# A hybrid decoder trunk: low-rank products in pairs on the two row halves, and wider small products at the mixers' seams

## The chip, the cores and the metric

The kernel runs on one core of one Trainium2 chip. The metric is the time of one execution on the device, in microseconds (us). TensorE (PE) multiplies, VectorE (DVE) and ScalarE (ACT) work elementwise, GpSimd (POOL) and SyncE (SP) mostly issue transfers. Products land in the banks of PSUM; everything else is in SBUF or in device memory.

## The reference

Two layers; each is a half-step SwiGLU block, a mixer and another half-step SwiGLU block, with a layer norm after each, on 16 learned tokens and 512 input tokens of width 1024. The mixer adds a convolution branch and an RWKV-7 branch. The part that the change touches, cut to what matters:

```python
def _rwkv_branch(zr, time_mix, w0, w_up, a0, a_up, g_up, k_k, k_a, r_k, lnx_g, lnx_b, wo):
    zr = zr + (_shift(zr) - zr) * time_mix
    r, k, v, zw, za, zg = jnp.split(zr, ...)       # 3 x 1024, then 64, 64, 128 columns
    w = -jax.nn.softplus(-(w0 + jnp.tanh(zw) @ w_up)) - 0.5
    decay = jnp.exp(-jnp.exp(w))                   # = exp(-0.6065 * sigmoid(w0 + ...))
    a = jax.nn.sigmoid(a0 + za @ a_up)             # the rate
    g = jax.nn.sigmoid(zg) @ g_up                  # the gate
    kk = normalised per head (k * k_k)
    k = k * (1.0 + (a - 1.0) * k_a)
    # per head and token, S is 64 x 64:
    #   sa = -S kk ; S = S * decay + sa (kk a)^T + v k^T ; y = S r
    ...
    return y @ wo
```

## The kernel before

Activations stand transposed: 128 partitions hold a slice of the width, the 528 tokens lie along the free dimension, in two halves of 264. Every large product is split into three of type float32r (high x high, high x low, low x high), each with 128 x 128 weights and 264 columns; lines L217 (SwiGLU, output projections) and L246 (input projection of the mixer) issue them. Float32 products have two records each in the trace, a float32r product has one.

The mixer (`mixer`) runs as follows. `mixer_begin` makes the low-rank inputs, then the **low-rank products**: decay (`w_up`, 64 rows, partitions 0 to 63), rate (`a_up`, 64 rows, partitions 64 to 127) and gate (`g_up`, 128 rows), eight output slices `o` each, for two halves of the tokens. One call of `lowrank` is one of them for one `o`: six products, then the evacuation from PSUM (a Sigmoid or Tanh on ACT, a scaling on DVE), then a store. Calls take turns between the two banks of the tile `sc` (emptied by one instruction of 528 columns) and the banks `tr` and `ch` (two of 264). The list LOW sets their order: decay and gate in turn, then the rate. Between them, after every fourth, comes a `filler`: one of the large input projections that the later stages need, whose inputs are ready, so that PE has work.

Then the recurrence, by head quarters q = 0 to 3, in chunks of 64 tokens. `prep` makes the factors (L1144: sums of squares per head, 128 rows, 32 columns; L1156 and L1157: transposes; L1205), `scores` the chunks' score matrices (L1250, L1259: 64 x 128 weights on the two row halves in turn, each half into a bank of its own), `substitution` inverts 16 x 16 blocks on DVE, `inverse` joins them to 64 x 64 (L1333, L1340; the last two of its three rounds L1340 take 32 columns), `meta` does the 16 learned tokens (L1365, L1371, L1459: 16 rows of `small`), `scan` walks through the chunks (L1415, L1428, L1431, L1436). Fillers and convolution taps stand between these. **Seam** here means the place between two quarters, where `inverse`, `meta` and the `prep` after the next stand together.

Engines work in the order of their own queue. The recorded program is reordered by a scheduler that knows priorities and modelled durations, so a change of one instruction moves others.

Of the kernel before, what the change touches and what calls it, by code (L numbers as in the profile page):

```python
# [7 lines left out]
F32 = mybir.dt.float32  # L8
F32R = mybir.dt.float32r
I32 = mybir.dt.int32  # L10
AF = mybir.ActivationFunctionType
# [5 lines left out]
P = 128  # L17
# [3 lines left out]
NM = 16  # L21
# [19 lines left out]
TAIL = 3  # L41
JTAIL = 4
HEAD = 2
LOW = [(j, o) for o in range(8) for j in (0, 2)] + [(1, o) for o in range(8)]
GNACT = ()
YR = (0, 3, 6)
CV = (0, 4, 7, 8)
# [51 lines left out]
class Trunk:  # L99
# [237 lines left out]
    def layer_vectors(self, l, room, mm):  # L337
        nc, lp = self.nc, self.lp
        y, ssum, sq = room
        nat, tmn = ssum[:, 0:P], ssum[0:26, P:2 * P]  # L340

        def fetch(out, src):
            self.nosync(nc.sync.dma_start(out=out, in_=src), self.issued)

        for i, nme in enumerate(VECS):
            src = self.d[nme][l]
            if nme == "r_k":
                src = src.rearrange("h n -> (h n)")
            fetch(nat[i * KT:(i + 1) * KT, :], src.rearrange("(o p) -> o p", p=P))
            if i % 4 == 3:  # L350
                yield True
        fetch(tmn, self.d["time_mix"][l].rearrange("(o p) -> o p", p=P))
        cwn = ssum[0:4 * TAPS, 2 * P:4 * P].rearrange("a (g p) -> a g p", p=P)
        for o in range(KT):
            g, i = divmod(o, 4)
            fetch(cwn[i * TAPS:(i + 1) * TAPS, g], self.d["conv_w"][l][:, o * P:(o + 1) * P])
            if o == 3:
                yield True
        yield True
        vec = lp.tile([P, P], F32, name="vec")  # L360
        ps = mm()
        nc.tensor.transpose(ps[:, 0:P], nat, self.ident)
        nc.tensor.transpose(ps[:, P:P + 26], tmn, self.ident[:26, :26])
        nc.scalar.copy(vec, ps[:, :P])
        tm = lp.tile([P, 26], F32, name="tm")
        nc.scalar.copy(tm, ps[:, P:P + 26])
        omtm = lp.tile([P, 26], F32, name="omtm")
        nc.vector.tensor_scalar(omtm, tm, -1.0, 1.0, op0=ALU.mult, op1=ALU.add)
        ps = mm()
        for g in range(2):  # L370
            nc.tensor.transpose(ps[:, 4 * g * TAPS:4 * (g + 1) * TAPS], cwn[:, g],
                                self.ident[:4 * TAPS, :4 * TAPS])
        cw = lp.tile([P, KT, TAPS], F32, name="cw")
        nc.scalar.mul(cw.rearrange("p o t -> p (o t)"), ps[:, :KT * TAPS], 0.5)
        v8 = lambda x: vec[:, VECS.index(x) * KT:(VECS.index(x) + 1) * KT]
        nkk = lp.tile([P, KT], F32, name="nkk")
        nc.vector.tensor_scalar_mul(nkk, v8("k_k"), -1.0)
        omka = lp.tile([P, KT], F32, name="omka")
        nc.vector.tensor_scalar(omka, v8("k_a"), -0.5, 1.0,
                                op0=ALU.mult, op1=ALU.add)  # L380
        half = lp.tile([P, 2, KT], F32, name="half")
        for i, x in enumerate(("a0", "k_a")):
            nc.vector.tensor_scalar_mul(half[:, i], v8(x), 0.5)
        self.layers.append((vec, tm, omtm, cw, nkk, omka, half))

# [582 lines left out]
    def mixer_begin(self, zs, filler):  # L968
# [14 lines left out]
        nc.vector.scalar_tensor_tensor(xg[1], z, 1.0, xg[0].bitcast(F32), op0=ALU.add,  # L983
                                       op1=ALU.subtract)
        filler(START[0])
        acts = (lambda o: (AF.Sigmoid, self.v1("w0", o), 1.0),
                lambda o: (AF.Tanh, self.half[:, 0, o:o + 1], 0.5))
        up = [(d["w_up"], slice(0, 64)), (d["a_up"], slice(64, P))]

        room = mp.tile([P, 4, KT, P], F32R, name="sb", bufs=1)  # L990
# [1 line left out]
                       dst=[room[:, 0], room[:, 1]])  # L992

        self.bi = 0
        stage = {}

        def lowrank(w, x, o, r, dst, act=None):
            if act is None:
                t = self.tmp("v", 4) if o % 2 else mp.tile([P, NCH * 4, 32], F32, name="b4",
                                                           bufs=B4)  # L1000
                t = t if o % 2 else t.rearrange("p a b -> p (a b)")[:, 0:T]
            else:
                if o == 0:
                    stage[r.start] = self.rows().rearrange("p q e f t -> p (q e f) t")
                t = stage[r.start][:, o]
            both = self.sc() if self.bi % 2 == 0 else None
            self.bi += 1
            for h in range(2):
                s = slice(h * (T // 2), (h + 1) * (T // 2))
                pm = (self.sm(("tr", "ch")[h]) if both is None else both[:, h])[:, :T // 2]  # L1010
                for j, (a, b) in enumerate(((0, 0), (0, 1), (1, 0))):
                    nc.tensor.matmul(pm, w[a][r, o, :], x[b][r, s], start=j == 0, stop=j == 2)
                to = t[:, s]
                if both is not None:
                    if h == 0:
                        continue
                    pm, to = self.pv(both), self.tv(t)
                if act is None:
                    nc.vector.tensor_scalar_mul(to, pm, 0.5)
                else:  # L1020
                    f, b, scale = act(o)
                    nc.scalar.activation(to, pm, f, bias=b, scale=scale)
            nc.sync.dma_start(out=dst[o * P:(o + 1) * P, :], in_=t)

        wg = self.wunit(d["g_up"][self.l].rearrange("r (o c) -> r o c", c=P),
                        dst=[room[:, 2], room[:, 3]])
        todo = [[lambda o=o, r=r, act=act, dst=dst: lowrank(w, x, o, r, dst, act)
                 for o in range(KT)]
                for (_, r), act, dst in zip(up, acts, (self.ds, self.as_))]
        todo.append([lambda o=o: lowrank(wg, xg, o, slice(0, P), self.ggs) for o in range(KT)])  # L1030
        for i, (j, o) in enumerate(LOW):
            todo[j][o]()
            if i % LOWSTEP == LOWSTEP - 1:
                filler(1)
            self.taps(TAP0[0])
        filler(START[1])
        self.sb = mp.tile([P, NCH, 4, 2 * C], F32, name="sb", bufs=1)

        self.ut = mp.tile([P, NCH * 2, C], F32, name="ut")

        small = mp.tile([NM, 2048], F32, name="small")
        self.small, o = {}, 0
        for name, n in (("kb", 512), ("s", 256), ("v", 256), ("u", 256), ("y0", 256), ("y1", 256), ("y2", 256)):
            self.small[name] = small[:, o:o + n]
# [70 lines left out]
    def prep_pair(self, q, p, Q):  # L1115
# [22 lines left out]

        pn = self.sc()
        pn, p0 = pn[:, 0], pn[:, 1]  # L1140
        tr = p0[:, NM:NM + 160]
        for j in range(5):
            k0 = NM + j * P if j < 4 else 0
            nc.tensor.matmul(tr[:, 32 * j:32 * j + 32], sq[:, k0:k0 + P], self.bones[:, ::4],  # L1144
                             start=True, stop=True)
        tr = tr[:, ::16]
        rs = mp.tile([P, 10], F32, name="rs", bufs=1)
        rx = self.tmp()[:, :4 * P].rearrange("p (j h v) -> p j h v", j=4, h=2)
        rx0 = mp.tile([P, P], F32, name="rx", bufs=1)[0:NM].rearrange("a (h v) -> a h v", h=2)
# [64 lines left out]
    def scores(self, q, Q):  # L1214
# [7 lines left out]
                nc.tensor.transpose(tr[0:NM, f * 256 + p * P:f * 256 + (p + 1) * P],  # L1222
                                    FB[p][:, f * NM:(f + 1) * NM], self.ident)
        kb0 = self.small["kb"]
        nc.scalar.copy(kb0, tr[0:NM, :])
        Q["kb0"] = kb0.rearrange("p (f h v) -> p f h v", f=2, h=4)
        ps = self.sc()
        ps = [ps[:, 0], ps[:, 1]]
# [2 lines left out]
        for e in range(2):  # L1231
            p0 = ps[e][0:NM, 0:4 * 2 * NM].rearrange("a (p f x) -> a p f x", p=2, f=2)
            r = slice(HS * e, HS * e + HS)
            for p in range(2):
                for f in range(2):
                    nc.tensor.matmul(p0[:, p, f, :], FB[p][r, f * NM:(f + 1) * NM],
                                     G[r, p, 1, :, 0:NM], start=True, stop=True)
            nc.vector.tensor_tensor(s0[:, e].rearrange("a p f g t -> a (p f) g t"),
                                    ps[e][0:NM, 0:4 * 2 * NM]
                                    .rearrange("a (x g t) -> a x g t", g=2, t=NM),  # L1240
                                    self.msk0[:, None].to_broadcast([NM, 4, 2, NM]), op=ALU.mult)
            nc.sync.dma_start(out=self.ms0[q, e::2].rearrange("h j t -> j h t"),
                              in_=s0[:, e, :, 1, 0, :])
        yield
        for c in range(NCH):
            cs = slice(NM + c * C, NM + (c + 1) * C)
# [70 lines left out]
    def inverse(self, q, g, Q):  # L1317
# [18 lines left out]
        for c0 in (0, 2 * NM, 2 * NM):  # L1336
            cs = slice(c0, C)
            for i in range(N):
                for r in halves:
                    nc.tensor.matmul(ps[r, i, cs], vt[r, i], x[r, i, cs], start=True, stop=True)  # L1340
            nc.vector.tensor_tensor(y[:, :, cs], ps[:, :, cs], dt[:, :, cs], op=ALU.add)
            x = y
        out = Q["G"].rearrange("a p e f t -> a (p e) f t")
# [9 lines left out]
    def meta(self, q, Q):  # L1353
# [4 lines left out]
        for p in range(2):  # L1358
            nc.tensor.transpose(tr[0:NM, p * P:(p + 1) * P], Q["v"][p][:, 0:NM], self.ident)
        v0 = hc(self.small["v"])  # L1360
        nc.scalar.copy(v0, hc(tr[0:NM, 0:256]))
        s0, kb0 = Q["s0"], Q["kb0"]
        ch = self.sm("ch")
        for h in range(4):
            nc.tensor.matmul(ch[0:NM, h * HS:(h + 1) * HS], s0[:, h % 2, h // 2, 0, 0, :],  # L1365
                             v0[:, h, :], start=True, stop=True)
        sa0 = hc(self.small["u"])
        nc.scalar.copy(sa0, hc(ch[0:NM, 0:256]))
        ch = self.sm("ch")
        for h in range(4):  # L1370
            nc.tensor.matmul(ch[0:NM, h * HS:(h + 1) * HS], xt0[:, h, :], sa0[:, h, :],  # L1371
                             start=True, stop=True)
        nc.scalar.copy(sa0, hc(ch[0:NM, 0:256]))
        ch = self.sm("ch")
        self.pairs([(ch[HS:P, h * HS:(h + 1) * HS], kb0[:, 0, h, :], v0[:, h, :],
                     kb0[:, 1, h, :], sa0[:, h, :]) for h in range(4)])
# [4 lines left out]
        if not self.last:  # L1381
# [1 line left out]
            self.pairs([(ch[0:NM, h * HS:(h + 1) * HS], s0[:, h % 2, h // 2, 0, 1, :], v0[:, h, :],  # L1383
                         s0[:, h % 2, h // 2, 1, 1, :], sa0[:, h, :]) for h in range(4)])
            y0 = self.small[f"y{q % 3}"].rearrange("a (m h v) -> a m h v", m=1, h=4)
            nc.scalar.copy(y0[:, 0], hc(ch[0:NM, 0:256]))
            Q["y0"] = y0

    def scan(self, q, Q):

# [378 lines left out]
```

## Time and profile before

| | |
|---|---|
| median of three runs | 3079.33 us (3071.02 to 3081.82) |
| the profiled execution | 3072.55 us |
| its span, first to last instruction | 3070.8 us |
| mean granted PE clock | 0.982 |
| busy: PE, DVE, ACT, POOL | 2996.3, 2276.7, 1439.3, 178.3 us |

The durations below come from the one profiled execution. A PE instruction is busy in the profile from its start until its result has landed, some 0.2 to 0.4 us, so consecutive ones overlap; how fast PE works is seen in the distance from start to start. In a merged row of the timeline, "x8" are eight records. The granted clock says what share of its full clock PE was given.

### The profile page before, as it was taken

To read this page: it belongs to the slowest core of one execution; us is meant where nothing else is said; L and a number is where in the kernel's file an instruction comes from. 1 tells how busy PE (TensorE), PEld (TensorE's weight loads), DVE (VectorE), ACT (ScalarE), POOL (GpSimd) and SP (SyncE) were. 2 spreads that over 40 slices of the span, in tenths; PEclk is the share of its full clock that TensorE was granted. 3 is DMA by queue.
4 is the path that set the end of the run, shared out by engine and by line. 5 is a ranking of instruction groups with operands and counts; after the bars stand their busy time and mean duration, and the time that the engine had idled before them with its cause. 6 is when DMAs were issued, how large, how long until landed. Compare 5 with 4: busy or idle time off the path is not lost. (4 is left out here: it accounts for less than half of the span.)

```text
span 3070.8 us, 64144 instructions
## 1 busy us (share of the span) xinstructions
PE 2996.3 (98%) x26076; PEld 2875.1 (94%) x26076; DVE 2276.7 (74%) x4689; ACT 1439.3 (47%) x2553; POOL 178.3 (6%) x286
## 2 busy tenths in 40 slices
PE   9999999999999999999999999999999999999998
PEld 9999989889888899999999999998889889999998
DVE  5766777788876768676776768778988748677767
ACT  4544464344455535444444444543454545254443
POOL 0110000000000000000001100000000000001100
PEclk9999999899999999999999999999999989999999
DMA  7665444335465554565545654443354645556652
GB/s 197 145 145 130 117 141 144 88 82 130 106 148 139 164 150 124 133 154 124 128 128 141 142 136 112 153 134 97 86 141 105 150 118 175 148 124 148 151 139 62
DMA packets 556149, 405.29 MB, mean 132 GB/s; under 512 B 89306, under 2 KB 500798, under 8 KB 555854
## 3 DMA queue, kind: packets, MB, share of 16 engines
q1 hardware_dynamic: 520302, 308.49, 35.2%
q0 software_dynamic: 30944, 84.18, 14.9%
q10 hardware_dynamic: 4608, 8.52, 0.7%
q8 instruction: 205, 3.36, 0.5%
q14 instruction: 90, 0.74, 0.1%
HBM read 270.81 MB, written 47.12 MB: 104 GB/s over the span
## 5 line engine op out<-in xcount | busy, mean ns | idle before, releaser
L217 PE MATMUL mm<-xh,w_hi 128*128 128x264 f32 (+1 forms) x1792 | 510.3, 286 | 7.5 <-ACT xh L460 5.9
L217 PE MATMUL mm<-xl,w_hi 128*128 128x264 f32 (+1 forms) x1792 | 509.1, 284 | 0.7 <-DVE xl L461 0.3
L217 PE MATMUL mm<-xh,w_lo 128*128 128x264 f32 (+1 forms) x1792 | 507.7, 284 | 0.0
L217 PE MATMUL mm<-hh,w_hi 128*128 128x264 f32 (+1 forms) x1408 | 399.7, 284 | 2.6 <-ACT hh L112 2.6
L217 PE MATMUL mm<-hh,w_lo 128*128 128x264 f32 (+1 forms) x1408 | 399.8, 284 | 0.0
L217 PE MATMUL mm<-hl,w_hi 128*128 128x264 f32 (+1 forms) x1408 | 399.5, 284 | 0.2
L246 PE MATMUL mm<-xh,w_hi 128*128 128x264 f32 x1760 | 388.8, 298 | 7.2 <-DVE kp L962 3.8
L246 PE MATMUL mm<-xh,w_lo 128*128 128x264 f32 x1760 | 384.1, 296 | 6.5 <-DMA w_lo<-w_raw 6.1
L246 PE MATMUL mm<-xl,w_hi 128*128 128x264 f32 x1760 | 386.6, 296 | 0.0
L1088 DVE SCALAR_TENSOR_TENSOR cacc<-cu,cw,cacc 128x528 f32<-128x528 f32 (+1 forms) x480 | 355.6, 754 | 3.5
L217 PEld LDWEIGHTS mm<-xh,w_hi 128*128 128x128 f32 x1792 | 337.1, 189 | 11.4 <-ACT xh L460 8.5
L217 PEld LDWEIGHTS mm<-xl,w_hi 128*128 128x128 f32 x1792 | 339.0, 189 | 2.7 <-DVE xl L461 2.5
L217 PEld LDWEIGHTS mm<-xh,w_lo 128*128 128x128 f32 x1792 | 338.7, 189 | 0.0
L122 ACT CAST w_hi<-sums 128x512 fp32r<-128x512 f32 (+1 forms) x204 | 155.0, 760 | 314.6 <-PE mm L217 202.7
L246 PEld LDWEIGHTS mm<-xh,w_hi 128*128 128x128 f32 x1760 | 284.5, 194 | 15.2 <-DVE kp L962 4.3
L246 PEld LDWEIGHTS mm<-xh,w_lo 128*128 128x128 f32 x1760 | 283.1, 194 | 14.0 <-DMA w_lo<-w_raw 7.5
L246 PEld LDWEIGHTS mm<-xl,w_hi 128*128 128x128 f32 x1760 | 283.4, 193 | 6.0
L217 PEld LDWEIGHTS mm<-hh,w_hi 128*128 128x128 f32 x1408 | 264.8, 188 | 3.2 <-ACT hh L112 3.0
L217 PEld LDWEIGHTS mm<-hl,w_hi 128*128 128x128 f32 x1408 | 265.0, 188 | 0.9 <-DVE hl L113 0.8
L217 PEld LDWEIGHTS mm<-hh,w_lo 128*128 128x128 f32 x1408 | 265.5, 189 | 0.1
L160 DVE TENSOR_TENSOR w_lo<-w_raw,w_hi 128x1024 fp32r<-128x1024 f32 (+1 forms) x194 | 204.2, 1055 | 74.5 <-ACT w_hi L149 70.0
L149 ACT CAST w_hi<-w_raw 128x1024 fp32r<-128x1024 f32 x134 | 140.6, 1051 | 247.2 <-PE mm L246 81.2
(366 smaller groups left out, 6819.9 us busy)
## 6 DMA issues: line engine op xcount, KB each, us to landing
w_raw<-in_w_in_dram SPq DMA_DIRECT2D x116, 512.0 KB
w_lo<-w_raw POOLq DMA_DIRECT2D x100, 512.0 KB, 4.9
w_raw<-in_ffn_wg_dram SPq DMA_DIRECT2D x88, 512.0 KB
w_raw<-in_ffn_wu_dram SPq DMA_DIRECT2D x88, 512.0 KB
w_raw<-in_ffn_wd_dram SPq DMA_DIRECT2D x80, 512.0 KB
w_lo<-w_raw POOLq DMA_DIRECT2D x68, 256.0 KB, 3.4
w_raw<-in_rwkv_wo_dram SPq DMA_DIRECT2D x16, 512.0 KB
w_raw<-in_conv_wo_dram SPq DMA_DIRECT2D x16, 512.0 KB
```

Source lines behind the costliest of these rows:

```text
L122: self.nc.scalar.copy(hi, x)
L149: copy = self.nc.scalar.copy(hi[:, :kt], raw[:, :kt])
L160: sub = self.nc.vector.tensor_tensor(lo[:, k], raw[:, k], hi[:, k].bitcast(F32), op=ALU.subtract)
L217: self.issued = self.nc.tensor.matmul(pm, a[:, k, :], b[:, xk + k, s], start=first and k == 0 and j == 0, stop=last and k == nk - 1 and j ...
L246: m = self.issued = nc.tensor.matmul(pm[:, h, :n], a[:, wk + k, :], b[:, xk + k, s:s + n], start=first and k == 0 and j == 0, stop=last an ...
L1088: tap = nc.vector.scalar_tensor_tensor(y, x, w, y, op0=ALU.mult, op1=ALU.add)
```

## The change

Decay and rate are now made in one step, `pair(o)`, and the gate in `single(o)`; the steps alternate for o = 0 to 7. In `pair`, for each half of the tokens, the products of decay (rows 0 to 63) and of rate (rows 64 to 127) stand in turn, each with a bank of its own: two banks (`sc`, or `tr` and `ch`) for each half of the tokens. A manual order keeps them in turn. Decay's Sigmoid becomes a Tanh of half the argument, and a Copy that scales and shifts; both outputs are emptied in halves of 264 columns.

At the seams: `small`, the tile of the learned tokens, has 128 partitions in place of 16, zeroed once a layer on POOL, so that L1365 and L1459 take 128 rows; the later two rounds of L1340 multiply all 64 columns, of which 32 are read; L1144 takes 64 columns in place of 32, of which every 32nd is read.

```diff
-LOW = [(j, o) for o in range(8) for j in (0, 2)] + [(1, o) for o in range(8)]
...
+        def banks():
+            self.bi ^= 1
+            if self.bi:
+                both = self.sc()
+                return both, [both[:, h] for h in range(2)]
+            return None, [self.sm(n) for n in ("tr", "ch")]
+
+        def pair(o):
...
+            for h in range(2):
+                pms = [x[:, :T // 2] for x in banks()[1]]
+                chain = []
                 for j, (a, b) in enumerate(((0, 0), (0, 1), (1, 0))):
...
+                    for pm, (_, r) in zip(pms, up):
+                        chain.append(nc.tensor.matmul(pm, w[a][r, o, :], halves(x[b])[h][r],
+                                                      start=j == 0, stop=j == 2))
+                for later, earlier in zip(chain[1:], chain):
+                    self.nosync(later, earlier)
+                for t, pm, i in ((tw, pms[0], 2), (ta, pms[1], 0)):
+                    nc.scalar.activation(halves(t)[h], pm, AF.Tanh,
+                                         bias=self.half[:, i, o:o + 1], scale=0.5)
+            nc.scalar.activation(tw, tw, AF.Copy, bias=0.5, scale=0.5)
...
+        for o in range(KT):
+            for step, n in ((pair, 2), (single, 1)):
+                step(o)
+                i += n
+                if i // LOWSTEP > (i - n) // LOWSTEP:
+                    filler(1)
...
-        small = mp.tile([NM, 2048], F32, name="small")
+        small = mp.tile([P, 2048], F32, name="small")
+        nc.gpsimd.memset(small, 0.0)
...
-            nc.tensor.matmul(tr[:, 32 * j:32 * j + 32], sq[:, k0:k0 + P], self.bones[:, ::4],
+            nc.tensor.matmul(tr[:, 64 * j:64 * j + 64], sq[:, k0:k0 + P], self.bones[:, ::2],
                              start=True, stop=True)
-        tr = tr[:, ::16]
+        tr = tr[:, ::32]
...
-                    nc.tensor.matmul(ps[r, i, cs], vt[r, i], x[r, i, cs], start=True, stop=True)
+                    nc.tensor.matmul(ps[r, i], vt[r, i], x[r, i], start=True, stop=True)
...
-            nc.tensor.matmul(ch[0:NM, h * HS:(h + 1) * HS], xt0[:, h, :], sa0[:, h, :],
+            nc.tensor.matmul(ch[0:NM, h * HS:(h + 1) * HS], xt0[:, h, :], sa0[0:NM, h, :],
                              start=True, stop=True)
```

How the instructions stand, on PE at the start of layer 0's low-rank products. Before (`kp`, `k` are the high and low part of the input of decay and rate, `a`, `pinv` those of the gate, `sb` the weights; sc, tr, ch are the banks):

```order
L246 MATMUL mm<-xh,w_lo 128x264 x2
L1012 MATMUL sc<-kp,sb 128x264
L1012 MATMUL sc<-k_4940,sb 128x264
L1012 MATMUL sc<-kp,sb 128x264 x2
L1012 MATMUL sc<-k_4940,sb 128x264
L1012 MATMUL sc<-kp,sb 128x264
L1012 MATMUL tr<-a,sb 128x264
L1012 MATMUL tr<-pinv,sb 128x264
L1012 MATMUL ch<-a,sb 128x264
```

After, the same place:

```order
L245 MATMUL mm<-xh,w_lo 128x264 x2
L1014 MATMUL sc<-kp,sb 128x264 x2
L1014 MATMUL sc<-k_4940,sb 128x264 x2
L1014 MATMUL sc<-kp,sb 128x264 x2
L1014 MATMUL tr<-kp,sb 128x264
L1014 MATMUL ch<-kp,sb 128x264
L1014 MATMUL tr<-k_4940,sb 128x264
L1014 MATMUL ch<-k_4940,sb 128x264
L1014 MATMUL tr<-kp,sb 128x264
L1014 MATMUL ch<-kp,sb 128x264
L1032 MATMUL sc<-a,sb 128x264
```

Each "x2" in bank sc is now one product of decay and one of rate; the second half of the tokens follows in tr and ch, and the gate comes back to sc.

On ACT, the evacuation of the same products. Before (`G` holds the outputs of decay, then of the rate; L149 casts weights, L1057 belongs to a filler):

```order
L1022 ACT_TABLE_LOAD
L1022 ACTIVATE G<-sc,vec 128x528 x2
L149 CAST w_hi<-w_raw 128x1024
L1022 ACTIVATE G<-sc,vec 128x528 x2
L1057 ACTIVATE glus<-mm 128x528
```

After:

```order
L1019 ACTIVATE G<-sc,half 128x264 x2
L1019 ACTIVATE G<-tr,half 128x264
L1019 ACTIVATE G<-ch,half 128x264
L1021 ACTIVATE G<-G 128x528
L1019 ACTIVATE G<-tr,half 128x264
L1019 ACTIVATE G<-ch,half 128x264
L148 CAST w_hi<-w_raw 128x1024
L1019 ACTIVATE G<-sc,half 128x264 x2
```

One evacuation of 528 columns has become four of 264 and a Copy within SBUF; the table loads between Sigmoid and the others are gone.

On PE at the seam of quarter 0 in layer 0 (`b` and `dd` are the blocks of `inverse`, `small` the learned tokens). Before:

```order
L1340 MATMUL sc<-dd,b_6679 64x64 x15
L1371 MATMUL ch<-small,xt 16x64 x4
L246 MATMUL mm<-xh,w_hi 128x264 x2
L246 MATMUL mm<-xl,w_hi 128x264 x2
L1340 MATMUL sc<-b_6679 64x32 x16
L1459 MATMUL ch<-small 64x64 x8
L246 MATMUL mm<-xh,w_lo 128x264 x2
L246 MATMUL mm<-xh,w_hi 128x264 x2
L1340 MATMUL sc<-b_6679 64x32 x16
L1459 MATMUL ch<-small 16x64 x8
L1144 MATMUL sc<-bones,tmp 128x32 x5
```

After (L1355 was L1340, L1386 was L1371, L1474 was L1459, L1159 was L1144):

```order
L1355 MATMUL sc<-dd,b_6696 64x64 x15
L1386 MATMUL ch<-small,xt 16x64 x4
L245 MATMUL mm<-xh,w_hi 128x264 x2
L245 MATMUL mm<-xl,w_hi 128x264 x2
L1355 MATMUL sc<-b_6696 64x64 x16
L1474 MATMUL ch<-small 64x64 x8
L245 MATMUL mm<-xh,w_lo 128x264 x2
L245 MATMUL mm<-xh,w_hi 128x264 x2
L245 MATMUL mm<-xl,w_hi 128x264
L1355 MATMUL sc<-b_6696 64x64 x16
L1474 MATMUL ch<-small 16x64 x8
L1159 MATMUL sc<-bones,tmp 128x64 x5
```

The order is the same but for one large product; the shapes are wider (that L1474 takes 128 rows stands in its operands, not in a row, which shows the output). Further on the scheduler interleaves scan and fillers in another order.

More of the change, by code (lines that the diff above doesn't have):

```diff
@@ L364, in layer_vectors @@
         nc.scalar.copy(vec, ps[:, :P])
-        tm = lp.tile([P, 26], F32, name="tm")
+        tms = lp.tile([P, 2, 26], F32, name="tm")
+        tm, omtm = tms[:, 0], tms[:, 1]
         nc.scalar.copy(tm, ps[:, P:P + 26])
-        omtm = lp.tile([P, 26], F32, name="omtm")
         nc.vector.tensor_scalar(omtm, tm, -1.0, 1.0, op0=ALU.mult, op1=ALU.add)
@@ L380, in layer_vectors @@
                                 op0=ALU.mult, op1=ALU.add)
-        half = lp.tile([P, 2, KT], F32, name="half")
-        for i, x in enumerate(("a0", "k_a")):
+        half = lp.tile([P, 3, KT], F32, name="half")
+        for i, x in enumerate(("a0", "k_a", "w0")):
             nc.vector.tensor_scalar_mul(half[:, i], v8(x), 0.5)
@@ L985, in mixer_begin @@
         filler(START[0])
-        acts = (lambda o: (AF.Sigmoid, self.v1("w0", o), 1.0),
-                lambda o: (AF.Tanh, self.half[:, 0, o:o + 1], 0.5))
         up = [(d["w_up"], slice(0, 64)), (d["a_up"], slice(64, P))]
@@ L994, in mixer_begin @@
         self.bi = 0
[L995 to L1007, printed above, removed]
+        stage = []
@@ new lines, in halves @@
+        def halves(x):
+            return [x[:, h * (T // 2):(h + 1) * (T // 2)] for h in range(2)]
+        def banks():
[5 more added lines that the diff above has]
+        def pair(o):
+            if o == 0:
+                for _ in up:
+                    stage.append(self.rows().rearrange("p q e f t -> p (q e f) t"))
+            tw, ta = (x[:, o] for x in stage)
@@ L1008, in lowrank @@
             for h in range(2):
-                s = slice(h * (T // 2), (h + 1) * (T // 2))
-                pm = (self.sm(("tr", "ch")[h]) if both is None else both[:, h])[:, :T // 2]
+                pms = [x[:, :T // 2] for x in banks()[1]]
+                chain = []
                 for j, (a, b) in enumerate(((0, 0), (0, 1), (1, 0))):
[L1012 to L1023, printed above, removed]
+                    for pm, (_, r) in zip(pms, up):
+                        chain.append(nc.tensor.matmul(pm, w[a][r, o, :], halves(x[b])[h][r],
+                                                      start=j == 0, stop=j == 2))
@@ new lines, in pair @@
+                for later, earlier in zip(chain[1:], chain):
[4 more added lines that the diff above has]
+            nc.scalar.activation(tw, tw, AF.Copy, bias=0.5, scale=0.5)
+            for t, dst in ((tw, self.ds), (ta, self.as_)):
+                nc.sync.dma_start(out=dst[o * P:(o + 1) * P, :], in_=t)
@@ new lines, in single @@
+        def single(o):
+            t = self.tmp("v", 4) if o % 2 else mp.tile([P, NCH * 4, 32], F32, name="b4", bufs=B4)
+            t = t if o % 2 else t.rearrange("p a b -> p (a b)")[:, 0:T]
+            both, pms = banks()
+            for h, pm in enumerate(pms):
+                pm = pm[:, :T // 2]
+                for j, (a, b) in enumerate(((0, 0), (0, 1), (1, 0))):
+                    nc.tensor.matmul(pm, wg[a][:, o, :], halves(xg[b])[h],
+                                     start=j == 0, stop=j == 2)
+                if both is None:
+                    nc.vector.tensor_scalar_mul(halves(t)[h], pm, 0.5)
+            if both is not None:
+                nc.vector.tensor_scalar_mul(self.tv(t), self.pv(both), 0.5)
+            nc.sync.dma_start(out=self.ggs[o * P:(o + 1) * P, :], in_=t)
@@ L1025, in mixer_begin @@
         wg = self.wunit(d["g_up"][self.l].rearrange("r (o c) -> r o c", c=P),
                         dst=[room[:, 2], room[:, 3]])
[L1027 to L1035, printed above, removed]
+        i = 0
@@ L1036, in mixer_begin @@
+        for o in range(KT):
[4 more added lines that the diff above has]
+                    filler(1)
+                self.taps(n * TAP0[0])
         filler(START[1])
@@ L1140, in prep_pair @@
         pn, p0 = pn[:, 0], pn[:, 1]
-        tr = p0[:, NM:NM + 160]
+        tr = p0[:, NM:NM + 320]
         for j in range(5):
             k0 = NM + j * P if j < 4 else 0
-            nc.tensor.matmul(tr[:, 32 * j:32 * j + 32], sq[:, k0:k0 + P], self.bones[:, ::4],
+            nc.tensor.matmul(tr[:, 64 * j:64 * j + 64], sq[:, k0:k0 + P], self.bones[:, ::2],
                              start=True, stop=True)
-        tr = tr[:, ::16]
+        tr = tr[:, ::32]
         rs = mp.tile([P, 10], F32, name="rs", bufs=1)
@@ L1224, in scores @@
         kb0 = self.small["kb"]
-        nc.scalar.copy(kb0, tr[0:NM, :])
+        nc.scalar.copy(kb0[0:NM], tr[0:NM, :])
         Q["kb0"] = kb0.rearrange("p (f h v) -> p f h v", f=2, h=4)
@@ L1237, in scores @@
                                      G[r, p, 1, :, 0:NM], start=True, stop=True)
-            nc.vector.tensor_tensor(s0[:, e].rearrange("a p f g t -> a (p f) g t"),
+            nc.vector.tensor_tensor(s0[0:NM, e].rearrange("a p f g t -> a (p f) g t"),
                                     ps[e][0:NM, 0:4 * 2 * NM]
@@ L1242, in scores @@
             nc.sync.dma_start(out=self.ms0[q, e::2].rearrange("h j t -> j h t"),
-                              in_=s0[:, e, :, 1, 0, :])
+                              in_=s0[0:NM, e, :, 1, 0, :])
         yield
@@ L1360, in meta @@
         v0 = hc(self.small["v"])
-        nc.scalar.copy(v0, hc(tr[0:NM, 0:256]))
+        nc.scalar.copy(v0[0:NM], hc(tr[0:NM, 0:256]))
         s0, kb0 = Q["s0"], Q["kb0"]
@@ L1367, in meta @@
         sa0 = hc(self.small["u"])
-        nc.scalar.copy(sa0, hc(ch[0:NM, 0:256]))
+        nc.scalar.copy(sa0[0:NM], hc(ch[0:NM, 0:256]))
         ch = self.sm("ch")
         for h in range(4):
-            nc.tensor.matmul(ch[0:NM, h * HS:(h + 1) * HS], xt0[:, h, :], sa0[:, h, :],
+            nc.tensor.matmul(ch[0:NM, h * HS:(h + 1) * HS], xt0[:, h, :], sa0[0:NM, h, :],
                              start=True, stop=True)
-        nc.scalar.copy(sa0, hc(ch[0:NM, 0:256]))
+        nc.scalar.copy(sa0[0:NM], hc(ch[0:NM, 0:256]))
         ch = self.sm("ch")
@@ L1385, in meta @@
             y0 = self.small[f"y{q % 3}"].rearrange("a (m h v) -> a m h v", m=1, h=4)
-            nc.scalar.copy(y0[:, 0], hc(ch[0:NM, 0:256]))
-            Q["y0"] = y0
+            nc.scalar.copy(y0[0:NM, 0], hc(ch[0:NM, 0:256]))
+            Q["y0"] = y0[0:NM]
     def scan(self, q, Q):
```

## The prediction

> **What bounds the kernel now.** I read the page first, then the busy time by stretches, then TensorE's (PE's) timeline at the two places that the change touches.
>
> ```profile
> PE 2996.3 (98%) x26076; PEld 2875.1 (94%) x26076; DVE 2276.7 (74%) x4689; ACT 1439.3 (47%) x2553; POOL 178.3 (6%) x286
> PEclk9999999899999999999999999999999989999999
> ```
>
> PE is busy for 98% of the span, and the other engines have room. But a busy PE is not a PE at full speed: the clock row has an 8 among the 40 slices of each mixer. The same by stretches (span in us, busy time and count of PE, its weight loads, DVE, ACT, POOL; then the granted clock, the DMA share, GB/s), for the mixers of layer 0 and 1:
>
> ```profile
> 356.00:1042.00 686.00, 656.19 (x6212) 603.26 (x6211) 533.52 (x1268) 317.41 (x614) 24.86 (x61) 0.96 0.46 124
> 1916.00:2570.00 654.00, 628.97 (x5979) 578.86 (x5980) 503.60 (x1162) 306.40 (x597) 24.89 (x61) 0.97 0.48 128
> ```
>
> So the mixers lose time in two ways: 55 us of idle PE in the two together, and a clock of 0.96 and 0.97. I looked for the stretches at half clock. Four of them begin just behind a seam, where the small products of one head quarter (inverse and meta) end; here is the window ahead of each, then the stretch itself, then two windows like them after which the clock stayed full:
>
> ```profile
> 577.70:581.10 3.40, 3.40 (x62) 3.04 (x59) 1.87 (x8) 0.36 (x1) 0.00 (x0) 1.00 1.11 313
> 823.50:826.90 3.40, 3.40 (x79) 3.05 (x79) 2.44 (x9) 1.87 (x3) 0.00 (x0) 1.00 0.49 138
> 2345.80:2349.20 3.40, 3.40 (x73) 3.15 (x74) 1.46 (x6) 0.00 (x0) 0.00 (x0) 1.00 1.13 312
> 2458.50:2461.90 3.40, 3.40 (x69) 3.05 (x66) 2.69 (x6) 0.36 (x1) 0.00 (x0) 1.00 1.05 283
> 581.10:591.40 10.30, 10.30 (x79) 9.80 (x79) 4.93 (x29) 3.21 (x6) 0.00 (x0) 0.50 0.06 20
> 826.90:837.20 10.30, 10.30 (x60) 10.04 (x58) 6.53 (x28) 3.45 (x7) 0.00 (x0) 0.50 0.18 52
> 2349.20:2356.00 6.80, 6.80 (x47) 6.74 (x44) 2.89 (x20) 2.03 (x4) 0.00 (x0) 0.50 0.04 13
> 2461.90:2472.10 10.20, 10.20 (x85) 9.31 (x84) 4.84 (x20) 4.02 (x9) 0.00 (x0) 0.50 0.15 56
> 942.90:946.30 3.40, 3.40 (x80) 3.07 (x79) 2.83 (x9) 1.23 (x2) 0.00 (x0) 1.00 0.18 65
> 2110.30:2113.70 3.40, 3.40 (x73) 3.15 (x75) 1.91 (x8) 1.05 (x1) 0.00 (x0) 1.00 0.69 213
> ```
>
> The four stretches sum to 37.6 us at clock 0.50, with PE busy in all of it. What is peculiar ahead of them isn't idleness: PE is busy 3.40 of 3.40 us. The timeline of the first seam (start, length, line, output<-inputs, rows*columns of the weights, input) shows what it did:
>
> ```profile
> 577.48 0.61 PE L1371 MATMUL ch<-small,xt 16*16 16x64 f32 x8
> 578.02 0.51 PE L246 MATMUL mm<-xh,w_hi 128*128 128x264 f32 x2
> 578.37 0.41 PE L246 MATMUL mm<-xl,w_hi 128*128 128x264 f32 x2
> 578.71 1.12 PE L1340 MATMUL sc<-b 64*64 64x32 f32 x32
> 579.76 1.14 PE L1459 MATMUL ch<-small 16*64 16x64 f32 x16
> 580.83 0.58 PE L246 MATMUL mm<-xh,w_lo 128*128 128x264 f32 x2
> 581.78 1.92 PE L1340 MATMUL sc<-b 64*64 64x32 f32 x32
> 583.63 1.88 PE L1459 MATMUL ch<-small 16*16 16x64 f32 x16
> 585.44 2.34 PE L1144 MATMUL sc<-bones,tmp 128*128 128x32 f32 x10
> 589.06 0.64 PE L246 MATMUL mm<-xl,w_hi 128*128 128x264 f32 x2
> 589.50 0.64 PE L246 MATMUL mm<-xh,w_lo 128*128 128x264 f32 x2
> 591.56 0.41 PE L246 MATMUL mm<-xl,w_hi 128*128 128x264 f32 x2
> 591.80 0.41 PE L246 MATMUL mm<-xh,w_lo 128*128 128x264 f32 x2
> ```
>
> Two of the large products take 0.44 us at half clock (589.06 to 589.50) and 0.24 us at full (591.56 to 591.80).
>
> My reading, an estimate: what counts is how many rows of the array take in data for how long. Four float32 records of 128 columns last 0.60 us (594.50, below), the last of them about 0.28 like other products, so one is 0.107 us; in proportion 64 columns are 0.053 and 32 are 0.027. I take it that such a record passes its columns twice and a large product its 264 once, which gives the latter 0.107 x 264/256 = 0.11 us. The window ahead of the stretch then holds 6 x 0.11 + 32 x 0.027 x 64/128 + 16 x 0.053 x 16/128 + some 0.02 for L1371 = 1.22 of 3.4 us: 0.36. The same sum over all records of the windows (x62, x79, x73, x69) gives 0.36, 0.32, 0.36, 0.34, and for the two that kept the clock 0.37 and 0.38 (x80, x73). So the limit lies near 0.365, and the seams stand right on it.
>
> **The low-rank products.** Before, 144 products a layer follow one another (L1012), those of decay and rate on 64 rows:
>
> ```profile
> 417.56 0.41 PE L1012 MATMUL sc<-kp,sb 64*128 64x264 f32 x2
> 417.81 0.28 PE L1012 MATMUL sc<-k,sb 64*128 64x264 f32 x1
> 417.93 0.28 PE L1012 MATMUL sc<-kp,sb 64*128 64x264 f32 x1
> 418.14 0.39 PE L1012 MATMUL tr<-a,sb 128*128 128x264 f32 x1
> 418.36 0.28 PE L1012 MATMUL tr<-pinv,sb 128*128 128x264 f32 x1
> ```
>
> One starts every 0.122 us, so a product on half the rows costs as much as one on all. A change of shape costs 0.21 - 0.12 = 0.09 at the change, and the next start comes 0.10 late as well (418.14 to 418.36): 0.19 us. Does a pair on the two row halves overlap? The trace has such pairs elsewhere, in the scores (L1259), besides four ordinary ones of the same 128 columns (L1156):
>
> ```profile
> 549.62 0.71 PE L1259 MATMUL sc<-G,FB 64*128 64x128 f32 x8
> 594.50 0.60 PE L1156 MATMUL sc<-ident,tmp 128*128 128x128 f32 x4
> L1259 PE MATMUL sc<-G,FB x512: 272/272/580, 529.8 to 2438.6; 64*128 64x128 f32 x171
> ```
>
> Eight records start within 0.71 - 0.27 = 0.44 us, where seven steps of 0.107 would be 0.75: they run two at a time. After, the 96 products of decay and rate of a layer are 48 such pairs: 48 x 0.122 x 2 layers = **-11.7 us**. Bounds: 0 (no overlap) and -11.7.
>
> In the changed order I count 56 changes of shape next to low-rank products against 48: 8 x 0.19 = **+1.6 us**.
>
> New waits: a pair must now be emptied by ACT in halves. ACT's and DVE's evictions stand in the trace (min/median/max ns):
>
> ```profile
> L1022 ACT ACTIVATE G<-sc,half x8: 699/702/707, 457.1 to 2001.4; 128x528 f32<-128x528 f32 x8
> L1022 ACT ACTIVATE G<-tr,half x8: 474/476/488, 457.7 to 2002.0; 128x264 f32<-128x264 f32 x8
> L149 ACT CAST w_hi<-w_raw 128x1024 fp32r<-128x1024 f32 x134 | 140.6, 1051 | 247.2 <-PE mm L246 81.2
> ```
>
> A step o costs ACT 4 x 0.476 + about 0.70 (the Copy of 528 columns, set equal to the eviction of 528) = 2.6 us, PE 12/2 x 0.122 + 6 x 0.122 + 2 x 0.19 = 1.84 us. What hides the rest is the large product pairs of the filler, 48 x 0.12 = 5.8 us each, six a layer. The first five groups stand without a filler: there the single of o = 0 needs bank sc, which waits for two Tanh, some 0.3 (product to eviction) + 0.95 us after the pair's first half, of which the second half covers 0.4. Two or three such waits make 1.5 us a layer: **+3 us**, bounds 0 and 6. The table loads that go (8 x 1.28 us on ACT, x8 of L1022) are worth nothing by themselves, for PE hardly waited for ACT there. The low-rank part in sum: -7.1 us.
>
> **The seams.** L1365 and L1459 take 128 rows for 16, most of them zeros; L1340 and L1144 twice the columns. L1144 and L1459 keep their spacing, since 10 records in 2.34 us at half clock (0.23 each) are far above what 32 or 64 columns stream: no cost. L1340 might pay:
>
> ```profile
> L1340 PE MATMUL sc<-b 64*64 64x32 f32 x1024 | 38.1, 226 | 0.0
> L1340 PE MATMUL sc<-dd,b 64*64 64x64 f32 x512 | 22.2, 222 | 1.1 <-issue 0.9 <-DVE b L1334 0.2
> ```
>
> 38.1/1024 = 0.037 against 22.2/512 = 0.043 us: at most 1024 x 0.006 = 6.3 us, at least 0; 30 to 32 records at 64 and at 32 columns take the same 1.1 us at the seam, so I take **+2**. The scheduler now interleaves more finely: 19 further changes of shape outside the low-rank part, **+3.6** (0 to 3.6, where the other row half or an idle PE hides them).
>
> The gain: with 64 columns at L1340 and 128 rows at L1459 the window of 577.7 holds 0.66 + 0.85 + 0.85 = 2.36 us, 0.69 of it, and the other three come to 0.78, 0.79 and 0.65, far above 0.365. If the stretches keep full clock, 37.6 us shrink by 0.12/0.22, to 20.5: -17.1. Part of this is waiting that remains; I take **-14**, bounds -17 and 0. The memset of small runs on POOL, at 6%, ahead of its first use: 0.
>
> Sum: -7.1 + 2 + 3.6 - 14 = **-15.5**, from the profiled execution's 3072.6 to 3057. The median of the three runs, 3079.3, lies 6.8 above that execution; stretches at half clock that come and go could be the difference. I add 2 us: **3059**.
>
> **Rivals.** (a) The low windows wander: the half clock comes one window later, since behind two of the seams my sum for the next window stays at 0.30 to 0.36. Then half the gain is left: 3064, with the same 2 us 3066. For it: the limit is crossed elsewhere in the mixers too, where nothing is changed. Against: at full clock that next window fills up sooner.
>
> (b) The clock asks only whether PE is at work, not on how many rows. Then the wider products change nothing of it, and -7.1 + 5.6 = -1.5 leaves 3071 to 3073. Against: four windows busy 3.40 of 3.40 us that lost the clock. The Trainium skill has this rule (TensorE: Matmul & The Clock Gate, section "Why this matters for your kernels"): no idle gaps above some 3 us between bursts, and the clock stays. By that rule the sum would be the 3071 to 3073 above; the trace disagrees, as those four windows show.
>
> (c) Slower: ACT paces the low-rank stage. If PE can't run the fillers while pairs wait, each step lasts ACT's 2.6 us, which is what 18 x 0.122 + 0.38 took before, so the gain is nil, and the casts for the fillers' weights (1.05 us, six a layer) are waited for as well: +12.6 + 5.6, and no clock gained: 3091 to 3093. It decides where ACT's queue is over 5.8 us behind; at 47% busy it shouldn't be.
>
> (d) The halves don't overlap: 3057 + 11.7 = 3069 to 3071; L1259 speaks against it.
>
> **How the numbers follow.** Forecast 0.58, (a) 0.20, (b) 0.12, (c) 0.06, (d) 0.04. A measurement here tells 0.5% (15 us) from no change: faster is below 3063.9. Nearly all of the forecast and a third of (a) lie there: faster 0.63, same 0.32, slower 0.05 (the upper part of (c)). The range runs from all bounds at their best (-11.7 + 1.6 - 17.1: 3045) to just beyond (b) (3074).
>
> **What would show it.** After the change, L1014's records start in twos 0.12 us apart; the stretches of half clock behind the four seams are gone, and the mixers' clock is 0.98 or more; idle of PE ahead of L1014 and L1032 is under 3 us a layer. The forecast is wrong if half clock still follows windows that my sum puts above 0.6, or if PE waits for the Tanh evictions throughout.

## The result, and the profile after

| | before | after |
|---|---|---|
| median of six runs each | 3076.49 us (3071.02 to 3081.82) | 3051.41 us (3045.16 to 3053.20) |
| the profiled execution | 3072.55 us | 3050.69 us |
| its span | 3070.8 us | 3049.0 us |
| mean granted PE clock | 0.982 | 0.990 |

The ratio is 0.9915 (95% interval 0.9899 to 0.9930): 25 us faster, by less than 2% and clearly more than 0.5%. The forecast was 3059, the range 3045 to 3074.

The rows of the page that answer to those of before:

```profile
PE 2970.4 (97%) x26076; PEld 2846.2 (93%) x26076; DVE 2281.8 (75%) x4683; ACT 1429.7 (47%) x2577; POOL 181.5 (6%) x288
PEclk9999999999999999999999999999999999999999
```

PE has as many records as before and is busy for 26 us less; both slices of 8 in the clock row are gone. The mixers by stretches (columns as before, the ends moved with the work):

```profile
356.00:1034.00 678.00, 648.57 (x6206) 593.79 (x6205) 535.14 (x1264) 313.50 (x626) 26.59 (x62) 0.97 0.47 125
1908.00:2548.00 640.00, 609.52 (x5974) 557.91 (x5975) 504.95 (x1156) 302.60 (x609) 26.54 (x62) 0.99 0.48 131
```

The clock rose from 0.96 to 0.97 and from 0.97 to 0.99, and they take 8 and 14 us less, while PE's idle time went from 55 to 60 us. The first seam of layer 0, PE's timeline:

```profile
576.92 0.51 PE L245 MATMUL mm<-xh,w_hi 128*128 128x264 f32 x2
577.27 0.41 PE L245 MATMUL mm<-xl,w_hi 128*128 128x264 f32 x2
577.62 1.15 PE L1355 MATMUL sc<-b 64*64 64x64 f32 x32
578.69 1.15 PE L1474 MATMUL ch<-small 128*64 128x64 f32 x16
579.77 0.51 PE L245 MATMUL mm<-xh,w_lo 128*128 128x264 f32 x2
580.12 0.40 PE L245 MATMUL mm<-xh,w_hi 128*128 128x264 f32 x2
580.36 0.28 PE L245 MATMUL mm<-xl,w_hi 128*128 128x264 f32 x1
580.57 1.15 PE L1355 MATMUL sc<-b 64*64 64x64 f32 x32
581.65 1.07 PE L1474 MATMUL ch<-small 128*16 128x64 f32 x16
582.64 1.33 PE L1159 MATMUL sc<-bones,tmp 128*128 128x64 f32 x10
583.78 0.37 PE L245 MATMUL mm<-xl,w_hi 128*128 128x264 f32 x1
583.99 0.41 PE L245 MATMUL mm<-xh,w_lo 128*128 128x264 f32 x2
584.23 0.41 PE L245 MATMUL mm<-xh,w_hi 128*128 128x264 f32 x2
```

Read it against the timeline of before. The wider shapes cost next to nothing: 32 records of L1355 in 1.15 us where 32 narrow ones took 1.12, 16 of L1474 in 1.15 against 1.14. And the second half of the seam runs at full clock: L1355 in 1.15 (1.92 before), L1474 in 1.07 (1.88), L1159 in 1.33 (2.34), two large products every 0.24. The windows there and the next remaining stretch of half clock, 8 us later:

```profile
579.80:583.20 3.40, 3.40 (x59) 3.08 (x59) 2.79 (x12) 0.96 (x2) 0.00 (x0) 1.00 0.20 65
583.20:586.60 3.40, 3.40 (x30) 3.40 (x30) 2.71 (x16) 3.00 (x5) 0.00 (x0) 1.00 0.02 5
591.60:595.00 3.40, 1.51 (x12) 1.14 (x13) 3.12 (x7) 2.63 (x7) 0.42 (x2) 1.00 0.23 56
595.00:608.60 13.60, 13.14 (x66) 11.53 (x67) 10.09 (x24) 4.55 (x12) 0.16 (x2) 0.50 0.53 125
```

What is left begins behind waits: PE is busy for 1.51 of 3.40 us ahead of this stretch, and for 2.5 us or less ahead of each of the ten that remain in this trace.

The start of the low-rank stage, PE's timeline and then two of its waits (engine, line, releaser; us in total, times, longest):

```profile
417.47 0.39 PE L1014 MATMUL sc<-kp,sb 64*128 64x264 f32 x2
417.69 0.28 PE L1014 MATMUL sc<-k,sb 64*128 64x264 f32 x2
417.81 0.28 PE L1014 MATMUL sc<-kp,sb 64*128 64x264 f32 x2
417.94 0.28 PE L1014 MATMUL tr<-kp,sb 64*128 64x264 f32 x1
417.94 0.28 PE L1014 MATMUL ch<-kp,sb 64*128 64x264 f32 x1
418.06 0.28 PE L1014 MATMUL tr<-k,sb 64*128 64x264 f32 x1
418.07 0.28 PE L1014 MATMUL ch<-k,sb 64*128 64x264 f32 x1
418.19 0.28 PE L1014 MATMUL tr<-kp,sb 64*128 64x264 f32 x1
418.19 0.28 PE L1014 MATMUL ch<-kp,sb 64*128 64x264 f32 x1
419.05 0.39 PE L1032 MATMUL sc<-a,sb 128*128 128x264 f32 x1 [0.58 <-ACT G L1019]
```
```profile
PE sc L1014 <- DVE b L1037: 3.0, 4, 1.4
PE sc L1032 <- ACT G L1019: 1.8, 4, 0.6
```

Within a run of pairs two products start at once, every 0.12 us, as foreseen; and the first single waits for the Tanh evictions, as foreseen. Unforeseen are the waits of a pair for DVE (L1037, the emptying of the gate's bank). Of the signs that were named, the twos at L1014, the four lost stretches and the idle time (2.6 and 2.2 us a layer) came; the clock of 0.98 came in layer 1 (0.99), not in layer 0 (0.97).

### The profile page after: what moved, and what is told of

Read it like the earlier page. It is cut to its first block, busy times and chain, and to the rows that moved or that the text cites. A ratio compares the mean times of both kernels' runs of the same rounds, so it can differ in the third digit from the quotient of the medians.

```text
span 3049.0 us, 64174 instructions
## 1 busy us (share of the span) xinstructions
PE 2970.4 (97%) x26076; PEld 2846.2 (93%) x26076; DVE 2281.8 (75%) x4683; ACT 1429.7 (47%) x2577; POOL 181.5 (6%) x288
## 4 chain that ended last, share of the span: by engine, by line
PE 81%; DVE 8%; DMA 4%; ACT 3%; issue 2%; SPq 1%; ACTq 0%; DVEq 0%; POOLq 0%
PE mm L216 53%; PE mm L245 15%; PE ch L1451 2%; PE sc L1355 2%; DVE cacc L1103 1%; PE tr L1430 1%; PE ch L1443 1%; PE sc L1274 1%; DMA w_lo<-w_raw 1%; DVE w_lo L159 1%; DMA w_raw<-in_w_in_dram 1%; DVE ln_rstd L443 1%; DVE xl L460 1%; ACT w_hi L148 1%; PE sc L1348 0%
```

## The experiments

Each ratio is to the kernel before on the same chip. For the profiled execution of each, the time at half clock follows from span and mean clock: 2 x (1 - clock) x span, 110 us before and 61 after.

### The parts apart

Low-rank part alone (all edits at the seams undone):

```diff
-        small = mp.tile([P, 2048], F32, name="small")
+        small = mp.tile([NM, 2048], F32, name="small")
...
-                    nc.tensor.matmul(ps[r, i], vt[r, i], x[r, i], start=True, stop=True)
+                    nc.tensor.matmul(ps[r, i, cs], vt[r, i], x[r, i, cs], start=True, stop=True)
...
-            nc.tensor.matmul(tr[:, 64 * j:64 * j + 64], sq[:, k0:k0 + P], self.bones[:, ::2],
+            nc.tensor.matmul(tr[:, 32 * j:32 * j + 32], sq[:, k0:k0 + P], self.bones[:, ::4],
...
```

> The low-rank part of the change alone, seams as before. Theory 1 (the sum of the prediction: pairs -11.7, changes of shape and waits +4.6): 3069, clock 0.98. Theory 2 (the gain of the change is all clock; what the pairs save is given back in changes of shape and waits): 3074 to 3079, ratio to before 0.998 to 1.001, clock 0.98.

Measured: 3071.3 us, 0.9986 (0.9967 to 1.0006), clock 0.982. Between the two theories: some 5 us, not told apart from nothing. Its trace still shows the peculiar case, at the seam of another quarter:

```profile
700.40:703.80 3.40, 3.40 (x67) 3.06 (x66) 2.87 (x9) 0.79 (x1) 0.00 (x0) 1.00 0.53 154
703.80:707.20 3.40, 3.40 (x39) 3.10 (x39) 1.47 (x5) 0.85 (x2) 0.00 (x0) 0.50 0.57 159
```

The seams alone (the kernel before with `small` on 128 partitions, L1340 and L1144 wide; LOW and `lowrank` as they were):

> The wider products at the seams alone, low-rank products as before. Theory 1 (clock -14, wider L1340 and changes of shape +5.6): about 3068. Theory 2 (the clock brings all of it): 3050 to 3055, as the whole change, and no half clock behind the four seams.

Measured: 3043.4 us, 0.9891 (0.9860 to 0.9921), clock 0.993. The seams bring all of the gain, even some us more than theory 2 had it (3050 to 3055), and none of the half clock that is left follows a seam with PE busy throughout. Its mixers:

```profile
356.00:1022.00 666.00, 641.33 (x6222) 589.01 (x6221) 534.91 (x1268) 316.70 (x614) 26.60 (x62) 0.99 0.47 128
1896.00:2541.00 645.00, 619.80 (x5974) 569.29 (x5975) 504.67 (x1161) 306.91 (x597) 26.67 (x62) 0.98 0.48 129
```

Layer 0 is 12 us shorter and layer 1 is 5 us longer than in the whole change. So this kernel was run again beside it:

> The wider seams alone, once more, beside the whole change on the same chip. If the low-rank part costs something on top of the seams: 3040 to 3046, 5 to 10 us under the whole change. If the first difference was chance: within 3 us of it.

> The whole change, once more, beside the wider seams alone on the same chip: 3047 to 3054 by its first six runs.

Measured: 3045.4 us, 0.9897 (0.9864 to 0.9930), clock 0.992, against 3049.9, 0.9910 (0.9882 to 0.9938), clock 0.989. The difference has the same sign and is 4.5 us now, between the two expectations; the intervals overlap, so that the low-rank part costs something on top is likely, not shown. Nothing here shows that it adds to the gain.

### Which of the edits at the seams

The learned tokens on 128 rows alone:

```diff
-        small = mp.tile([NM, 2048], F32, name="small")
+        small = mp.tile([P, 2048], F32, name="small")
+        nc.gpsimd.memset(small, 0.0)
...
```

> Only the tile of the learned tokens on 128 partitions (L1365, L1459); L1340 and L1144 narrow as before. By the row sum the windows ahead of the four stretches rise to 0.57, 0.56, 0.58 and 0.52, above 0.365, so most of the gain at the seams: 3053 to 3062, clock 0.985 or more. By the theory that the clock asks only whether PE is busy: no change, 3074 to 3079, clock 0.98.

Measured: 3062.0 us, 0.9956 (0.9940 to 0.9971), clock 0.987. The busy theory falls: the same products with the same spacing (at full clock a record of L1459 starts every 61.5 ns on 16 rows and on 128), on rows that hold zeros, take 14 us off.

The columns alone:

```diff
-            nc.tensor.matmul(tr[:, 32 * j:32 * j + 32], sq[:, k0:k0 + P], self.bones[:, ::4],
+            nc.tensor.matmul(tr[:, 64 * j:64 * j + 64], sq[:, k0:k0 + P], self.bones[:, ::2],
...
-                    nc.tensor.matmul(ps[r, i, cs], vt[r, i], x[r, i, cs], start=True, stop=True)
+                    nc.tensor.matmul(ps[r, i], vt[r, i], x[r, i], start=True, stop=True)
```

> Only L1340 and L1144 with 64 columns; the learned tokens on 16 rows as before. By the row sum the four windows rise to 0.48, 0.54, 0.57 and 0.47, also above 0.365: 3055 to 3065, clock 0.985 or more, a little less than rows alone, since L1459 leaves later windows low. By the busy theory: 3074 to 3079 or, with a slower L1340, up to 6 more.

Measured: 3049.1 us, 0.9912 (0.9880 to 0.9944), clock 0.990: better than expected, and better than the rows alone, against my order of the two. With L1340 alone wide (only the second part of that diff):

> Only L1340 with all 64 columns; L1144 and the learned tokens as before. By the row sum the windows ahead of the four stretches rise by 0.13, 0.22, 0.20 and 0.13 to 0.48, 0.54, 0.57 and 0.47: as L1340 and L1144 together, 3046 to 3058. If L1144's columns carry the gain of the two: 3065 to 3077. If 64 columns at L1340 cost the 6.3 us of the upper bound, both are 4 us more.

Measured: 3057.9 us, 0.9941 (0.9917 to 0.9966), clock 0.987. So the rows alone are worth 14 us, L1340 alone 18, both columns 27, and all together 33: they don't add, as is to be expected if they lift the same windows over the same limit. The traces agree with that. Stretches of half clock behind a window in which PE was busy throughout number four before and four with the low-rank part alone; none with the rows alone, with both columns, with the seams or with the whole change; and one with L1340 alone. Why the gains still differ (14, 18, 27 and 33 us) was not taken apart; all other stretches follow windows with waits. That 64 columns at L1340 cost little is seen at full clock, where 32 records took 0.03 us more: 1 us over the 1024 of the group. In the changed kernel the whole group takes no more than the 38.1 us of before, part of which ran at half clock:

```profile
L1355 PE MATMUL sc<-b 64*64 64x64 f32 x1024 | 36.7, 221 | 0.0
```

### What the clock counts

The dummy products that keep PE at work during the norms, in the changed kernel, on 16 of 128 rows; nothing reads their results:

```diff
-            m = self.nc.tensor.matmul(ps, x, x[:, None, :].to_broadcast([P, 4, P]),
+            m = self.nc.tensor.matmul(ps, x[0:NM], x[0:NM, None, :].to_broadcast([NM, 4, P]),
```

> The changed kernel, but the dummy products that keep PE at work during the norms (L227 of before, 512 columns) use 16 of the 128 rows; their results are never read. They take as long as before. Row theory: to the clock they are 1/8 of the work, so half clock appears behind the norms: mean clock 0.97 to 0.98, 8 to 25 us more than the changed kernel (3060 to 3075). Busy theory: nothing changes, 3047 to 3055, clock 0.99.

Measured: 3077.2 us, 1.0004 (0.9987 to 1.0022), clock 0.979: 26 us more than the changed kernel, the whole gain gone, and 2 us more than the row theory expected at most. The timeline of such a stretch, and its windows:

```profile
989.13 7.41 PE L226 MATMUL sc<-ones 16*128 16x512 f32 x23
```
```profile
988.90:992.30 3.40, 3.40 (x20) 2.73 (x18) 1.84 (x4) 0.99 (x2) 0.00 (x0) 1.00 0.42 113
992.30:995.70 3.40, 3.40 (x10) 2.58 (x9) 2.96 (x14) 0.00 (x0) 0.00 (x0) 0.51 0.20 60
```

PE streams 512 columns without a gap and still loses its clock in the next window: the dummy products start every 0.23 us in one and every 0.43 in the next. The counterpart keeps all rows and takes 16 weight columns:

```diff
-            m = self.nc.tensor.matmul(ps, x, x[:, None, :].to_broadcast([P, 4, P]),
+            m = self.nc.tensor.matmul(ps[0:NM], x[:, 0:NM], x[:, None, :].to_broadcast([P, 4, P]),
```

> The changed kernel, but the same dummy products keep 128 rows and make only 16 output columns of the array (16 weights columns, 512 moving columns). If rows times time count: as the changed kernel, 3047 to 3055, clock 0.99. If the used area (rows times columns) counts: as with 16 rows, 3060 to 3075 and clock 0.97 to 0.98.

Measured: 3048.5 us, 0.9908 (0.9874 to 0.9942), clock 0.989, as the changed kernel. The same stretch:

```profile
991.82 7.10 PE L226 MATMUL sc<-ones 128*16 128x512 f32 x30
```
```profile
992.60:996.00 3.40, 3.40 (x17) 1.35 (x16) 2.47 (x7) 0.63 (x1) 0.00 (x0) 1.00 0.50 150
996.00:999.40 3.40, 3.40 (x19) 1.78 (x18) 2.20 (x11) 0.22 (x1) 0.00 (x0) 1.00 0.01 4
```

Rows count, columns of weights don't: the row sum, not the used area. I worked the row sum out for every window of all fourteen traces of this study (12 experiments, before, after); in each of them the clock changes at multiples of 3.41 us only, which gives the windows. With a product counted whole in the window in which it starts, and without the first 20 and the last 10 us of a trace, 173 stretches of half clock begin in them; the window ahead of each has a sum of 0.41 or less, of 158 of them 0.365 or less; only 3 windows under 0.365 kept the clock, each at 0.354.

These exceptions come from the counting. If a product is spread over its streaming time from 0.1 us after its start on (the delay that separates best), the windows ahead of all 201 stretches, both ends of the traces included, have 0.374 or less, and of the 12,013 windows at full clock that kept it one lies lower than 0.375, at 0.364. The same count separates far worse with another sum: with the streaming time alone, without the rows, at least 54 windows stand on the wrong side of any limit, and with rows times columns of weights 99.

### The low-rank products

Within a pair, first the three products of decay, then the three of rate:

```diff
-                for j, (a, b) in enumerate(((0, 0), (0, 1), (1, 0))):
-                    for pm, (_, r) in zip(pms, up):
+                for pm, (_, r) in zip(pms, up):
+                    for j, (a, b) in enumerate(((0, 0), (0, 1), (1, 0))):
```

> The changed kernel, but within a pair the three products of decay come first and then the three of rate, so that the row halves don't take turns. If the turns make the overlap and PE's time there counts: 96 x 0.122 = 11.7 us more than the changed kernel, some 3063. If what the turns save is waited away for evictions anyway: 3051 to 3055.

Measured: 3050.6 us, 0.9924 (0.9900 to 0.9948). This was meant to take the overlap away and did not. The program has kp, k, kp of decay in bank tr, then kp, k, kp of rate in ch; the timeline of PE shows

```profile
417.64 0.28 PE L1014 MATMUL tr<-kp,sb 64*128 64x264 f32 x1
417.65 0.28 PE L1014 MATMUL ch<-kp,sb 64*128 64x264 f32 x1
417.77 0.28 PE L1014 MATMUL tr<-k,sb 64*128 64x264 f32 x1
417.78 0.28 PE L1014 MATMUL ch<-k,sb 64*128 64x264 f32 x1
417.89 0.28 PE L1014 MATMUL tr<-kp,sb 64*128 64x264 f32 x1
```

in turn: PE starts the fourth product beside the first. So the order in the program isn't what makes the pairs, and this run says nothing of what the overlap is worth; its time lies at the edge of the second range, but not for the reason that was given there.

Last, fillers earlier: LOWSTEP from 4 to 3, so that 8 fillers stand among the low-rank products for 6, in the seams alone and in the whole change:

> The wider seams alone with a filler after every third low-rank group in place of every fourth (8 fillers there, 2 fewer later): no work is added, only the order behind the low-rank stage is shifted. Theory order (what the low-rank part costs on top is the order that the later stages happen to get): this too moves by several us, 3045 to 3055. Theory waits (the low-rank part costs by its own waits): as the seams alone, 3040 to 3046.

> The whole change with the same shift of fillers. Theory order: anywhere from 3040 to 3056, without regard to the low-rank products. Theory waits: more cover for the evictions, so 2 to 4 us under the whole change.

Measured: 3068.6 us, 0.9970 (0.9949 to 0.9991), clock 0.988, and 3065.9, 0.9956 (0.9936 to 0.9976), clock 0.986: 23 and 16 us more than with LOWSTEP 4, above either theory's range. In the traces of the seams alone (e8 and e11) the stage from the mixer's first large product to the first of the line that was L1144 grows by 13.3 and 12.4 us for its two more fillers; what follows gets no shorter in layer 0 (1442.1 us in both, to the next mixer) and 5 us shorter in layer 1. So fillers spent early are missed later, and that is worth more than all that the low-rank stage could save. It doesn't tell the two theories apart.

## Why the prediction was right, and where its sum was not

Direction, range and the mechanism of the clock held: 22 us between the profiled executions, of which -15.5 was foreseen, and 25 between the medians. By parts the sum was further off. The seams alone bring 33 and 32 us (e2, e8) for 8.4 foreseen (-14 + 2 + 3.6), and the low-rank part on top of them took back some 4 to 8 us, where 7.1 of gain was foreseen. The two errors offset each other, and that 3059 lies so near to 3051 is in part luck.

**The clock** (-14, bounds -17 and 0) was sized too small. The four stretches behind the seams are gone, as foreseen. But seams also fall into the grid of windows in other ways in other executions, and stretches that I didn't count went too: 110 us at half clock became 61. In the twelve traces with LOWSTEP 4 the span follows 3026 + 0.39 x (us at half clock) within 4 us; for 49 us less that is -19, nearly all of the 22. It is a fit over kernels that differ in other things as well; the two tests with dummy products, which are among the twelve, lie on it too, and the two traces with LOWSTEP 3 lie 4 and 9 us above it.

**The low-rank part** (-7.1) was sized too large. The pairs do overlap and the waits came (4.8 us in both layers for 3: 1.8 for the Tanh evictions that were foreseen, 3.0 for DVE, which were not), but from the mixer's first large product to the first of L1144 the stage went from 75.6 to 74.1 us in layer 0 and from 75.4 to 75.2 in layer 1. In the run of the part alone it went to 73.3 and 73.4, 4.3 us in both, about the 5 us by which that kernel's median is lower; with the pairs' products in the other program order (e5) it took 72.7 in both layers. Where the rest of the 7.1 went was not isolated. In layer 1 of the changed kernel its wait even cost the clock: pairs and one wait of 1.09 us leave the window low.

```profile
1962.78 0.39 PE L1014 MATMUL sc<-kp,sb 64*128 64x264 f32 x2 [1.09 <-DVE b L1037]
```
```profile
1960.30:1963.70 3.40, 2.16 (x19) 1.45 (x18) 3.40 (x5) 2.75 (x7) 0.00 (x0) 1.00 0.72 231
1963.70:1967.10 3.40, 3.40 (x16) 3.40 (x17) 3.10 (x7) 1.46 (x4) 0.00 (x0) 0.50 0.78 249
```

**L1340 wider** (+2): some 1 us. **Further changes of shape** (+3.6): not measured by themselves; outside the low-rank products the trace of the seams alone has 13 more of them than before and that of the whole change 23, and the former is the faster kernel, which agrees with a cost, without showing it.

**The rivals.** (b), the clock of a busy PE, fell with the 16-row products; its rule in the Trainium skill (TensorE: Matmul & The Clock Gate, section "Why this matters for your kernels") is not enough here, as a window that was busy for 3.40 of 3.40 us lost the clock. (a) fell: no stretch remains behind a seam with PE busy throughout; half clock remains behind waits, and the gain is larger than forecast, not half. (c) and (d) fell: waits of 4.8 us in all, and pairs that start together.

**Open:** why the low-rank part seems to bring some 5 us on the old seams and nothing, or a loss, on the new ones (neither difference is clear of noise). The traces put the difference behind the low-rank stage (more half clock and idle time in another order of scan and fillers); which part of that order does it wasn't isolated.

## What to carry to other kernels

A PE that is busy all the time can still run at half clock, where its products take few rows: read the granted clock by short windows, and sum rows times streaming time for each. Where the spacing of small products doesn't grow with rows or columns (here 32 records of L1340 took 1.12 us with 32 columns and 1.15 with 64, and L1459 the same on 16 and 128 rows), padding them with zero rows or unread columns costs next to nothing and keeps the clock. The best kernel of this study is the seams alone: 3043 to 3045 us, 0.989 to 0.990 of before.

## What the runs showed that I had not expected

The limit of the clock is sharp (a row sum of about 0.37 of a window of 3.4 us; 0.36 when a product is counted whole where it starts) and indifferent to weight columns: 16 of 128 left the clock at 0.989, 16 of 128 rows took it to 0.979. And PE doesn't keep to the program's order between the two row halves, though engines were said at the start to work in the order of their queue: in e5 the product that stood fourth started 0.01 us after the first.
